# Row gathers by indirect DMA in the gated experts of a three-layer model, conditioning in blocks of 1024 columns, and the overflow loop at the head of its stage

## The chip, the cores and the metric

One core of a Trainium2 chip runs the whole program. The metric is the device time of one execution in microseconds, lower is better. The kernel before takes 2925.19 us (median of 3 runs, 2920.35 to 2933.56).

## What is computed

512 tokens of width 1024 go through three layers. Each has a mixer over the sequence (RWKV-7 with gated linear attention, then RG-LRU with Hyena, then a conformer convolution) and, after it, a mixture of experts (MoE). The first MoE has 32 experts of width 512; each token takes two of them. The later two have 16 experts of width 1024, and there each expert chooses its 64 tokens:

```python
def _ec_moe(h, router, w1, w3, w2):
    probs = jax.nn.softmax(jnp.einsum('bnd,de->ben', h, router), axis=1)
    gates, idx = lax.top_k(probs, cap)           
    xs = h[bidx, idx]
    a = jnp.einsum('becd,edf->becf', xs, w1)
    g = jnp.einsum('becd,edf->becf', xs, w3)
    y = jnp.einsum('becf,efd->becd', jax.nn.silu(a) * g, w2) * gates[..., None]
    return jnp.zeros_like(h).at[bidx, idx].add(y)
```

The input `h` of these two is a normalised row times `1 + scale` plus `shift`. Scale, shift and an output gate come from the conditioning vector: `silu(c) @ w_mod + b_mod`, a 1024 by 6144 matrix for each of the two later layers. All arithmetic is float32.

## The kernel before

The program is written against a tile framework. It emits operations in program order, and a scheduler puts them into one fixed list per engine; an engine runs its own list strictly in order and waits on semaphores. Emission order is the priority, so that an operation emitted late fills places where earlier ones would wait by the scheduler's reckoning. Below, SP is the engine whose queue issues the weight loads, and POOL (GpSimd) issues the software DMAs and the gathers.

The stages in the profiled run: the first mixer until about 640 us (`phase1`; it also has the conditioning, as filler work), the first MoE until about 1335 (`moe1`; it also has the Hyena `filters` and the context recurrence, `context`, as filler), the second mixer until about 1640, the MoE of the first later layer until 2168.5 (`moe2`), the third mixer until 2380, and the MoE of the second later layer until about 2908.

**Conditioning** (`adaln_block`, L909 to L945). 48 blocks of 256 columns; each is two loads of 512 KB into `wm` (2 buffers), eight matmuls at L921 into four column groups of the array, a copy at L923, and one more matmul step with `sel` that adds up the four groups (L931 for gate rows, L937 for scale and shift). Among the blocks, `zeros` clears a `wm` tile and writes it nine times into the region of `yslot` (a DRAM table of expert outputs) that belongs to slots which nobody fills: one DMA of 4.6 MB on POOL's queue, L348.

**The first MoE** works in 16 pairs of experts. `tokens` (L1636) computes for two pairs at a time which token sits in which slot: one-hot (`oh`), eight small matmuls (`tr`, L1743), a reduction and a cast on VectorE (L1745, L1746). `rows_load` (L1748) then gathers 128 rows of `xrow` (normalised rows in DRAM) by one indirect DMA on POOL (`xg`, 512 KB, L1752) and transposes them on TensorE (`gat` and `cb`, L1757). `ffn` runs the gate and up products `G` (L1519), the transposes `tr` (L1529) and the down product `Y` (L1539). An expert with more than 64 tokens is finished in `overflow` (L1931), a hardware loop whose count is read at run time; in the profiled run the count is zero. It stands before pair 4, with nine weight tiles loaded ahead (`self.ahead(9)`), and the filters just before it. A hardware loop is entered by all engines together, once all DMAs in flight have landed.

**The later MoEs** work in four quads, each of two pairs of experts. `experts` (L1811) builds the one-hot `oh` of a quad. `gather` (L1488) multiplies all 512 normalised rows by it, 64 matmuls of 256 columns at L1496; the rows are held in SBUF as two parts, `xhi` and `xlo`, 16 KB each per partition, so that their sum is exact, and the result is already transposed; an activation (L956) applies scale and shift. Per pair follow the slots' gates (`slot_gates`, L1731), the transposed one-hot `ohT` (L1828), `ffn`, and `outputs` (L1773), which multiplies by the gate and spreads the result back to the tokens by `cb` matmuls (L1796) with `yhi` and `ylo`, and adds them to `xres`.

**Weights** come in tiles of 1 MiB through a ring of buffers; a load (`ring`, L1449) is issued from SP's queue when a buffer is free. A pair of the later MoEs takes 24 loads: 16 for `G`, 8 for `Y`; a layer takes 192. Ring of the later MoEs: 6 tiles that are there before the mixer's memory is free and 9 behind (5 and 10 in the last layer), 15 in all. `moe_open` and `ring_open` lay it out. Two names of the list below: an fp32 matmul with 512 columns in an engine's list (`G`, `Y`) is two instructions in the trace; `gat`, `cb` and the transposes are one.

Of the kernel before, what the change touches and what calls it, by code (L numbers as in the profile page):

```python
# [10 lines left out]
F32 = mybir.dt.float32  # L11
# [9 lines left out]
T, D = 512, 1024  # L21
# [158 lines left out]
class Kern:  # L180
# [57 lines left out]
    def phase1(self, _):  # L238
# [4 lines left out]
        with ExitStack() as es:  # L243
# [82 lines left out]
            def shifted(ft, out):  # L326
# [14 lines left out]
            self.adaln_setup(P, "glo")  # L341
            fills = (self.adaln_block(l, cb, lambda: P([128, 1024], "wm", bufs=2), lambda: bank("ad"), lambda: P([128, 256], "rows", bufs=2))
                     for l in range(2) for cb in range(24))
            def zeros():

                z = P([128, 1024], "wm", bufs=2)
                nc.gpsimd.memset(z, 0.0)
# [8 lines left out]
            fill(24)  # L356
            self.rwkv_pair(1, **X)
            gl(6)
            fill(10)
            self.rwkv_pair(2, **X)  # L360
            self.rwkv_pair(3, **X)
            fill(12)
# [501 lines left out]
    def norm_tile(self, M, W, bank, t, wr, ps_):  # L864
        nc, V = self.nc, self.nc.vector
        x = self.xres[:, t]
        hi, lo = (M.xn[t],) * 2 if M.rows else (M.hi[:, t], M.lo[:, t])
# [9 lines left out]
        nc.scalar.activation(lo, x, AF.Square, accum_out=rs)  # L877
        nc.scalar.activation(rs, rs, AF.Sqrt, scale=1.0 / D, bias=self.eps)
        V.reciprocal(rs, rs)
        if M.rows:  # L880
            V.scalar_tensor_tensor(hi, x, rs, M.lnrow, op0=OP.mult, op1=OP.mult)
            nc.gpsimd.dma_start(self.xrow[128 * t:128 * t + 128], hi)
            return
        nc.scalar.activation(hi, x, AF.Copy, scale=rs)
        V.scalar_tensor_tensor(lo, x, rs, hi.bitcast(F32), op0=OP.mult, op1=OP.subtract)
# [9 lines left out]
    def adaln_setup(self, p, tag="sel4"):  # L895
# [6 lines left out]
        sel4 = p([128, 128, 4], tag)[:, 0:32]  # L902
        nc.gpsimd.memset(sel4, 1.0)
        nc.gpsimd.affine_select(out=sel4, in_=sel4, pattern=[[-1, 32], [-32, 4]], compare_op=OP.is_equal, fill=0.0,
                                base=0, channel_multiplier=1)
        self.sel = p([128, 32], "sel")
        nc.vector.tensor_reduce(self.sel, sel4, axis=AX.X, op=OP.add)

    def adaln_block(self, l, cb, w4, bank, row):  # L909

        nc, c = self.nc, self.col
        ws = []
        for g in range(2):
            w = w4().rearrange("p (k n) -> p k n", k=4)
            nc.sync.dma_start(w, self.A["w_mod"][l, 512 * g:512 * g + 512, 256 * cb:256 * cb + 256]
                              .rearrange("(k p) n -> p k n", p=128))
            ws.append(w)
        ps = bank()
        for g in range(2):
# [3 lines left out]
        nc.scalar.copy(rows, ps[:, 0:256])  # L923
        j, part = divmod(cb, 4)
        ps = bank()
        if j in (2, 5):
            q = 2 * l + (j == 5)
            g = row()[0:1]
            z = self.gates[q:q + 1, 256 * part:256 * part + 256]
            nc.gpsimd.dma_start(g, self.A["b_gate"][q:q + 1, 256 * part:256 * part + 256])  # L930
            nc.tensor.matmul(ps[0:32, 0:256], self.sel, rows, start=True, stop=True)  # L931
            nc.vector.tensor_add(g, g, ps[0:1, 0:256])
            nc.gpsimd.dma_start(z, g)
            return
        p2 = ps[:, 0:4].rearrange("p (a b) -> p a b", b=2)
        for a in range(2):
            nc.tensor.matmul(p2[:, a], rows[:, 128 * a:128 * a + 128], self.sel[:, 0:2], start=True, stop=True)  # L937

        where = {0: 1, 1: 0, 3: 3, 4: 2}[j] + 6 * l
        todo = [(where, 0, j)]  # L940
        if l == 0 and j < 2:
            todo.append((4 + (j == 0), 1, j))
        for slot, m, j in todo:
            o = self.mods[:, slot, 2 * part:2 * part + 2]
            nc.vector.tensor_add(o, p2[:, :, m], c(f"b_mod{l}{j}", 2 * part, 2))  # L945
            if j in (1, 4):
                n = c(f"norm{1 if j == 1 else 2}_g_2{l}", 2 * part, 2)
# [540 lines left out]
    def gather(self, P, bank, hi, lo, oh, n, affine):  # L1488

        nc = self.nc  # L1490
        xT = P([128, KT, 256], "xT")[:, :, 0:n]
        for k in range(KT):
            ps = bank("gat", 1)[:, 0:n]
            for t in range(NT):
                for m, part in enumerate((hi, lo)):
                    nc.tensor.matmul(ps, part[:, t, 128 * k:128 * k + 128], oh[:, t], start=t == 0 and m == 0,  # L1496
                                     stop=t == NT - 1 and m == 1)
            affine(xT[:, k], ps, k)
        return xT

# [43 lines left out]
    def moe1(self, yT):  # L1544
        nc, tc, A = self.nc, self.tc, self.A
        with ExitStack() as es:
            c = self.col
            M, bank = self.moe_open(es, "m1", "right", True)
            self.ring_open(es, 9, "right")
            ring = self.rings[0][0]  # L1550
            M.xn = [z for i in range(2) for z in tiles(ring([128, 2, D], "w", bufs=9))]
            self.rings = [(ring, "w", 7, 9)]
# [14 lines left out]

            self.rings = self.rings + [(P, "w", 2, 2), (ring, "w", 2, 9)]
# [74 lines left out]

            tokens(0)

# [36 lines left out]
            def over():  # L1682
                self.ahead(9)
                self.overflow(P, B, bank, s1, s12, pend)

            bk = lambda: bank("bg", 1)
            for pair in range(15):
                if pair % 2 == 0 and pair < 14:
                    tokens(pair // 2 + 1)
                if pair == 4:  # L1690
                    self.filters(B, bk)
                    over()
                z = slice(128 * pair, 128 * pair + 128)
                self.rows_ffn(P, bank, self.rows_load(P, bank, tok[:, pair:pair + 1], 128), self.yslot[z], self.take, 2)
# [21 lines left out]
            for t in range(NT):  # L1716
                for n in range(2):
# [3 lines left out]
                    V.tensor_add(self.xres[:, t, z], self.xres[:, t, z], ps)  # L1721
            self.context(B, bk)

    def slot_gates(self, P, bank, oh, m, cols):

        nc = self.nc
        g = P([128, 1], "gate", bufs=2)
        ps = bank("tr", 1)
        for e in range(m // 64):
            for t in range(NT):  # L1730
                nc.tensor.matmul(ps[64 * e:64 * e + 64, 0:1], oh[:, t, 64 * e:64 * e + 64].bitcast(F32), cols(t, e),  # L1731
                                 start=t == 0, stop=t == NT - 1)
        nc.scalar.copy(g[:m], ps[:m, 0:1])
        return g
# [13 lines left out]
    def rows_load(self, P, bank, tok, m):  # L1748

        nc, V = self.nc, self.nc.vector  # L1750
        xg = P([128, D], "xg", bufs=3)[:m]
        nc.gpsimd.indirect_dma_start(xg, None, self.xrow[:], bass.IndirectOffsetOnAxis(ap=tok, axis=0))  # L1752
        xT = P([128, KT, 128], "xT", bufs=2)[:, :, 0:m]
        for b in range(2):
# [3 lines left out]
            (V.tensor_copy if b else nc.scalar.copy)(xT[:, 4 * b:4 * b + 4], ps)  # L1758
# [52 lines left out]
    def experts(self, P, bank, hi, lo, R, cm, affine, ne, ff, g2, at={}):  # L1811

        nc, V = self.nc, self.nc.vector
        for quad in range(ne // 4):
            if quad in at:
                at[quad]()
# [232 lines left out]
```

## Time and profile before

| | |
|---|---|
| median of 3 runs | 2925.19 us |
| the profiled execution | 2929.81 us, span 2928.2 us |
| TensorE busy | 2551.1 us (87%), mean granted clock 0.934 |
| VectorE, ScalarE, GpSimd busy | 38%, 23%, 3% of the span |
| DMA | 765.9 MB, mean 262 GB/s |
| bytes on the software queue (POOL's) | 28.92 MB |

Read it by stage: a mean over the span mixes stages in which the DMA engines stand half idle (the mixers) with stages in which they move about 400 GB/s without a pause (the MoEs). "Idle before, releaser" tells how long an engine stood idle before an instruction and what ended it. The granted clock is given as a share of full speed: 1.00 is 2.4 GHz, 0.50 is 1.2 GHz.

### The profile page before, as it was taken

How to read it: one execution, taken by the hardware profiler on the slowest of the kernel's cores; microseconds unless marked ns; L12 is line 12 of the kernel's file. 1: busy time of each engine (PE TensorE's matmuls, PEld its weight loads, DVE VectorE, ACT ScalarE, POOL GpSimd, SP SyncE). 2: the span in 40 equal slices, each digit the busy share in tenths (PEclk: the TensorE clock that was granted, in tenths of full speed). 3: DMA queues.
4: the chain of work that ended last, by engine and by line, in shares of the span. 5: the costliest groups of instructions: out<-in, count | busy, mean ns of one | idle time of the engine just before them, and what ended most of it. 6: DMA issues, size and time to landing. Idle time of an engine off the chain costs nothing.

```text
span 2928.2 us, 37470 instructions
## 1 busy us (share of the span) xinstructions
PE 2551.1 (87%) x15670; PEld 1395.8 (48%) x15670; DVE 1109.9 (38%) x2099; ACT 672.9 (23%) x1092; POOL 87.2 (3%) x169
## 2 busy tenths in 40 slices
PE   7989999867996988868889699999989669999997
PEld 3565756655433444435566533333347553333333
DVE  3857576734211230014776411111138651111113
ACT  3233323322101350004631211011024321101101
POOL 1000000000110000010000000000000000000000
PEclk9988999878998999988999799999999779999999
DMA  4345343137989999993133399999953238999987
GB/s 148 110 165 191 100 143 125 59 110 269 351 325 345 397 349 394 397 398 127 58 121 118 138 397 400 409 382 409 379 206 128 90 151 350 401 409 382 409 330 295
DMA packets 277963, 765.90 MB, mean 262 GB/s; under 512 B 15579, under 2 KB 66011, under 8 KB 276896
## 3 DMA queue, kind: packets, MB, share of 16 engines
q1 hardware_dynamic: 260480, 711.77, 64.4%
q0 software_dynamic: 8992, 28.92, 2.5%
q10 hardware_dynamic: 8320, 22.80, 2.2%
q8 instruction: 124, 2.03, 0.3%
q14 instruction: 47, 0.39, 0.0%
HBM read 740.34 MB, written 23.09 MB: 261 GB/s over the span
## 4 chain that ended last, share of the span: by engine, by line
PE 48%; DVE 8%; issue 5%; DMA 4%; ACT 3%; POOL 0%; DVEq 0%; POOLq 0%; ACTq 0%; SPq 0%
PE G L1519 19%; PE Y L1539 12%; PE b L1222 4%; PE gat L1496 3%; PE cb L1796 3%; PE G L809 2%; PE Y L809 2%; DMA xg<-xrow,tok 1%; DVE cy L1391 1%; PE tr L1529 1%; DMA w<-in_moe_w_up_dram 1%; DVE h L1524 1%; DMA yo<-yslot,slot 1%; PE tr L876 1%; PE b L1341 0%
## 5 line engine op out<-in xcount | busy, mean ns | idle before, releaser
L1519 PE MATMUL G<-w,xT 128*64 128x256 f32 (+1 forms) x4096 | 745.0, 496 | 17.9 <-DMA w<-in_moe_w_up_dram 11.8
L1519 PEld LDWEIGHTS G<-w,xT 128*64 128x64 f32 x4096 | 291.1, 138 | 375.1 <-issue 289.4
L1539 PE MATMUL Y<-w,hT 128*64 128x512 f32 x1536 | 452.1, 603 | 2.4 <-DMA w<-in_moe_w_down_dram 1.3
L1539 PEld LDWEIGHTS Y<-w,hT 128*64 128x64 f32 x1536 | 148.1, 137 | 227.3 <-issue 210.7
L1524 DVE TENSOR_TENSOR h<-h,G 128x256 f32<-128x256 f32 (+1 forms) x64 | 35.3, 552 | 530.1 <-PE G L1519 394.7
L1787 DVE SCALAR_TENSOR_TENSOR y<-Y,gate,g 128x512 f32<-128x512 f32 x32 | 24.0, 751 | 331.7 <-PE Y L1539 330.1
L1798 DVE TENSOR_TENSOR xres<-xres,cb 128x512 f32<-128x512 f32 x116 | 79.6, 686 | 101.0 <-PE cb L1796 101.0
L321 PE MATMUL mm<-hT,w 128*128 128x512 f32 x240 | 113.7, 609 | 0.0
L1523 ACT ACTIVATE h<-G 128x256 f32<-128x256 f32 (+1 forms) x64 | 31.4, 490 | 301.0 <-PE G L1519 288.9
L956 ACT ACTIVATE xT<-gat,mods 128x256 f32<-128x256 f32 x64 | 36.1, 563 | 247.4 <-PE gat L1496 207.2
L1222 PE MATMUL b<-big,wh 128*128 128x512 f32 x320 | 83.9, 414 | 5.6 <-ACT wh L861 3.0
L1530 ACT COPY hT<-tr 128x256 f32<-128x256 f32 (+1 forms) x64 | 30.6, 478 | 243.8 <-PE tr L1529 243.8
L921 PE MATMUL ad<-wm,sc 128*32 128x256 f32 x768 | 68.0, 416 | 18.7 <-DMA wm<-in_w_mod_dram 15.9
L1496 PE MATMUL gat<-oh,xhi 128*128 128x256 f32 x256 | 75.1, 321 | 7.7 <-ACT xT L956 4.0
L1788 ACT CAST yhi<-y 128x512 fp32r<-128x512 f32 x30 | 18.5, 618 | 265.6 <-DVE y L1787 164.0
L1496 PEld LDWEIGHTS gat<-oh,xhi 128*128 128x128 f32 x256 | 50.9, 199 | 51.0 <-issue 29.2
L1222 PEld LDWEIGHTS b<-big,wh 128*128 128x128 f32 x320 | 62.7, 198 | 23.5 <-ACT big L1203 6.4
L1796 PEld LDWEIGHTS cb<-yhi,ohT 128*128 128x128 f32 x114 | 21.2, 186 | 103.0 <-DVE xres L1798 56.8
L1496 PE MATMUL gat<-oh,xlo 128*128 128x256 f32 x256 | 67.9, 295 | 0.0
L643 PE MATMUL g<-wb,hT 128*64 128x128 f32 x1024 | 64.5, 275 | 3.5 <-DVE ga L718 2.1
L321 PEld LDWEIGHTS mm<-hT,w 128*128 128x128 f32 x240 | 42.3, 190 | 48.3 <-issue 47.4
L1796 PE MATMUL cb<-yhi,ohT 128*128 128x512 f32 x114 | 56.9, 499 | 9.7 <-ACT yhi L1788 9.7
(684 smaller groups left out, 3700.4 us busy)
## 6 DMA issues: line engine op xcount, KB each, us to landing
w<-in_exp_w_dram SPq DMA_DIRECT2D x384, 1024.0 KB, 12.7
w<-in_moe_w_gate_dram SPq DMA_DIRECT2D x64, 1024.0 KB, 15.4
w<-in_moe_w_up_dram SPq DMA_DIRECT2D x64, 1024.0 KB, 15.3
w<-in_moe_w_down_dram SPq DMA_DIRECT2D x64, 1024.0 KB, 13.9
wm<-in_w_mod_dram SPq DMA_DIRECT2D x96, 512.0 KB, 4.3
ws<-in_w_in_dram SPq DMA_DIRECT2D x20, 512.0 KB, 3.5
ws<-in_cf_w_dram SPq DMA_DIRECT2D x20, 512.0 KB, 3.5
st<-in_w_out_dram SPq DMA_DIRECT2D x16, 512.0 KB, 4.6
```

The lines of the kernel that those rows point to most:

```text
L321: nc.tensor.matmul(ps[:m], w[:, k, col0:col0 + m], hT[:, k], start=k == 0, stop=k == KT - 1)
L643: nc.tensor.matmul(ps[half[h], b], hT[:, k, 64 * j:64 * j + 64], w[h][:, k], start=k == 0, stop=k == KT - 1)
L809: nc.tensor.matmul(ps, a[:, k, z], b[:, k % 2], start=k == 0 and m == 0, stop=k == KT - 1 and m == 2)
L921: nc.tensor.matmul(ps[32 * k:32 * k + 32, 0:256], self.sc[:, 4 * g + k], ws[g][:, k], start=g == 0, stop=g == 1)
L956: self.nc.scalar.activation(out, ps, AF.Identity, scale=a, bias=b)
L1222: nc.tensor.matmul(ps, a[:, k], b[:, k], start=m == 0 and k == 0, stop=m == 2 and k == KT - 1)
L1496: nc.tensor.matmul(ps, part[:, t, 128 * k:128 * k + 128], oh[:, t], start=t == 0 and m == 0, stop=t == NT - 1 and m == 1)
L1519: nc.tensor.matmul(parts[m][64 * c:64 * c + 64], xT[:, k, 64 * e:64 * e + 64], w[:, kk, H * c:H * c + H], start=k == 0, stop=k == KT - 1)
L1524: nc.vector.tensor_mul(h, h, parts[1])
L1539: nc.tensor.matmul(ys[n][64 * e:64 * e + 64], hTs[e][:, f], ws[e][:, ff_, 512 * n:512 * n + 512], start=f == 0, stop=f == nf - 1)
L1796: nc.tensor.matmul(ps, ohT[:m, 128 * t:128 * t + 128], p[k][:m], start=k == 0, stop=k == 1)
L1798: V.tensor_add(xr, xr, ps)
```

## The change

There are three parts.

**The later experts gather rows by DMA.** `norm_tile` writes the normalised rows to `xrow` in DRAM (four POOL DMAs of 512 KB per layer) as the first MoE's already did, and `xhi` and `xlo` are gone. A new `prepare(pair)` computes the slots' token numbers and gates together (eight matmuls of three columns, a reduction, a cast), gathers 128 rows by indirect DMA, transposes them (8 transposes), applies scale and shift in 8 small operations (4 on ScalarE, 4 on VectorE), and builds `ohT`. It is called for the next pair ahead of `ffn`. The ring has 10 early tiles in place of 6 (9 for 5), of which two hold the rows until they are written, and 7 behind (8): 17 tiles in all.

**Conditioning in 12 blocks of 1024 columns**: eight loads of 512 KB each, each with four matmuls into the four column groups, which now hold four ranges of columns rather than four parts of a sum. So L931's step is gone, and L937's is 8 blocks of two matmuls.

**The first MoE**: the zeros are written just before `tokens(0)`, pair 0's rows are loaded before the loop, the loop stands before pair 0 with eleven tiles loaded ahead, and `filters` is emitted behind the pairs, just before `context`.

```diff
-            fills = (self.adaln_block(l, cb, lambda: P([128, 1024], "wm", bufs=2), lambda: bank("ad"), lambda: P([128, 256], "rows", bufs=2))
-                     for l in range(2) for cb in range(24))
-            def zeros():
...
-                nc.gpsimd.dma_start(self.yslot[1920:].rearrange("(a p) d -> p a d", p=128), z[:, None].to_broadcast([128, 9, 1024]))
-
-            fills = itertools.chain(itertools.islice(fills, 8), (zeros() for _ in range(1)), fills)
+            fills = (self.adaln_block(l, j, lambda: P([128, 1024], "wm", bufs=2), lambda: bank("ad"), lambda: P([128, 256], "rows", bufs=2))
+                     for l in range(2) for j in range(6))
...
-        for g in range(2):
-            for k in range(4):
-                nc.tensor.matmul(ps[32 * k:32 * k + 32, 0:256], self.sc[:, 4 * g + k], ws[g][:, k], start=g == 0, stop=g == 1)
+        for k in range(KT):
+            w = w4()
+            nc.sync.dma_start(w, self.A["w_mod"][l, 128 * k:128 * k + 128, D * j:D * j + D])
+            for g in range(4):
+                nc.tensor.matmul(ps[32 * g:32 * g + 32, 0:256], self.sc[:, k], w[:, 256 * g:256 * g + 256], start=k == 0,
+                                 stop=k == KT - 1, tile_position=(0, 32 * g))
...
+            z = P([128, D], "xg", bufs=3)
+            nc.gpsimd.memset(z, 0.0)
+            nc.gpsimd.dma_start(self.yslot[1920:].rearrange("(a p) d -> p a d", p=128), z[:, None].to_broadcast([128, 9, 1024]))
             tokens(0)
+            xT0 = self.rows_load(P, bank, tok[:, 0:1], 128)
...
-            def over():
-                self.ahead(9)
-                self.overflow(P, B, bank, s1, s12, pend)
-
+            self.ahead(11)
+            self.overflow(P, B, bank, s1, s12, pend)
...
-                if pair == 4:
-                    self.filters(B, bk)
-                    over()
...
+            self.filters(B, bk)
             self.context(B, bk)
...
+            ps = bank("bg", 1)
+            for e in range(2):
                 for t in range(NT):
...
+                    nc.tensor.matmul(ps[64 * e:64 * e + 64, 0:3], oh[:, t, e].bitcast(F32), gt[:, t, 2 * pair + e],
+                                     start=t == 0, stop=t == NT - 1)
+            g, tok = P([128, 2], "gate", bufs=3), P([128, 1], "tok", I32, bufs=2)
+            V.tensor_reduce(g[:, 1:2], ps[:, 1:3], axis=AX.X, op=OP.add)
+            V.tensor_copy(tok, g[:, 1:2])
+            nc.scalar.copy(g[:, 0:1], ps[:, 0:1])
+            xT = self.rows_load(P, bank, tok, 128, affine)
+            ps = bank("bg", 1)
...
+        nxt = prepare(0)
+        for pair in range(ne // 2):
+            xT, g, ohT = nxt
+            if 2 * pair + 2 < ne:
+                nxt = prepare(pair + 1)
+            ys = self.ffn(P, bank, xT, self.take, 2, ff)
+            self.outputs(P, bank, ys, g, 128, g2, ohT, 2 * pair + 2 == ne)
```

**Where instructions stand now.** TensorE's list of the kernel before, in the `Y` product of a pair whose next quad is gathered beside it (`Y` uses the weights `w` and the transposed hidden rows `hT`; `gat` gathers by `oh`):

```order
L1496 MATMUL gat_11572<-oh_11549,xlo_10550 128x256
L1828 MATMUL tr_11643<-identr_78,oh_11549 128x128 x3
L1539 MATMUL Y_11455<-w_11469,hT_11389 64x512
L1539 MATMUL Y_11456<-w_11469,hT_11389 64x512
L1496 MATMUL gat_11582<-oh_11549,xhi_10549 128x256
L1496 MATMUL gat_11582<-oh_11549,xlo_10550 128x256
L1496 MATMUL gat_11582<-oh_11549,xhi_10549 128x256
L1496 MATMUL gat_11582<-oh_11549,xlo_10550 128x256
L1496 MATMUL gat_11582<-oh_11549,xhi_10549 128x256
L1496 MATMUL gat_11582<-oh_11549,xlo_10550 128x256
L1496 MATMUL gat_11582<-oh_11549,xhi_10549 128x256
L1496 MATMUL gat_11582<-oh_11549,xlo_10550 128x256
```

The gather's matmuls stand in eights between the steps of `Y`. TensorE's list of the changed kernel, in the `G` product of the third pair: the slots' numbers (`bg<-gt,oh`), `ohT` (`bg<-identr,oh`), and the first half of the transposes of the gathered rows (`gat<-ident,xg`); the rows `xg_11558` are those whose numbers the third row here computes.

```order
L1716 MATMUL cb_11312<-ident_72,xg_11300 128x128 x4
L1493 MATMUL G_11329<-w_11354,xT_11046 64x512 x3
L1789 MATMUL bg_11544<-gt_10725,oh_11542 64x3 x8
L1493 MATMUL G_11329<-w_11360,xT_11046 64x512 x4
L1798 MATMUL bg_11579<-identr_78,oh_11542 128x128 x4
L1493 MATMUL G_11329<-w_11366,xT_11046 64x512 x4
L1716 MATMUL gat_11561<-ident_72,xg_11558 128x128 x4
L1493 MATMUL G_11329<-w_11372,xT_11046 64x512 x4
L1503 MATMUL tr_11381<-ident_72,h_11378 128x128 x4
```

So between the numbers of a pair's tokens and the first instruction that reads the gathered rows stand eight matmuls of `G` and the four of `ohT`; the second half of the transposes (`cb<-ident,xg`) stands one pair later, and `Y` is 32 matmuls with nothing between. Each of the six gathers behind the first two has such a place; the first of them has six `cb` matmuls there as well.

POOL's list of the kernel before at the head of the first MoE (`xrow` are the normalised rows being written, `cpad` belongs to the context recurrence, `xg` are pair gathers):

```order
L882 DMA xrow<-w_5416 128x1024 x2
L882 DMA xrow<-w_5417 128x1024
L994 MEMSET cpad_8842 128x1
L995 MEMSET cpad_8842 128x2
L994 MEMSET cpad_8861 128x1
L995 MEMSET cpad_8861 128x2
L882 DMA xrow<-w_5417 128x1024
L1752 DMA xg_5979<-xrow,tok_5914 128x1024
L1752 DMA xg_6122<-xrow,tok_5914 128x1024
```

The same place in the changed kernel; `ovi` is the loop's count.

```order
L877 DMA xrow<-w_5138 128x1024 x2
L877 DMA xrow<-w_5139 128x1024
L1615 MEMSET xg_5637 128x1024
L981 MEMSET cpad_8567 128x1
L982 MEMSET cpad_8567 128x2
L981 MEMSET cpad_8586 128x1
L982 MEMSET cpad_8586 128x2
L1616 DMA yslot<-xg_5637 128x9x1024
L877 DMA xrow<-w_5139 128x1024
L1711 DMA xg_5654<-xrow,tok_5636 128x1024
L1929 TENSOR_LOAD ovi_5731
L1930 COMPARE_AND_BRANCH
```

The clearing of a tile and the write of zeros now stand ahead of the last write of `xrow` and of pair 0's gather, and the loop follows that gather; in SP's list it follows the eleventh weight load.

## Rows read from the trace of the kernel before

**Rows 1.** Windows: us, PE, PEld, DVE, ACT, POOL busy (x), PEclk, DMA share, GB/s

```profile
0.00:640.00 640.00, 556.81 (x6160) 365.52 (x6160) 394.47 (x890) 196.64 (x340) 27.65 (x65) 0.91 0.38 122
...
640.00:1335.00 695.00, 582.92 (x3341) 309.66 (x3342) 160.63 (x338) 138.58 (x235) 56.14 (x72) 0.93 0.94 351
...
1640.00:2168.50 528.50, 484.44 (x2146) 191.47 (x2146) 94.59 (x151) 55.89 (x99) 0.00 (x0) 0.97 0.94 370
...
2380.00:2908.00 528.00, 483.84 (x2150) 191.84 (x2150) 93.94 (x150) 55.89 (x99) 0.00 (x0) 0.97 0.94 373
```

**Rows 2.** Windows: two pairs of the first later layer, and all eight

```profile
1733.10:1802.45 69.35, 66.83 (x295) 26.73 (x296) 8.75 (x14) 8.85 (x16) 0.00 (x0) 1.00 1.03 409
1802.45:1860.60 58.15, 55.26 (x246) 20.09 (x248) 10.82 (x16) 4.34 (x8) 0.00 (x0) 1.00 1.01 398
...
1684.30:2168.50 484.20, 464.77 (x2045) 176.97 (x2044) 72.77 (x104) 48.61 (x87) 0.00 (x0) 1.00 0.97 383
```

**Rows 3.** Groups by line in 1684.3 to 2168.5: busy us, mean ns | idle before

```profile
L1496 PE MATMUL gat<-oh,xhi 128*128 128x256 f32 x103 | 28.7, 308 | 2.0 <-ACT xT L956 2.0
...
L1496 PE MATMUL gat<-oh,xlo 128*128 128x256 f32 x104 | 26.3, 286 | 0.0
```

**Rows 4.** Timeline of TensorE: start us, us, instruction [idle before <-releaser]

```profile
1733.05 1.94 PE L1519 MATMUL G<-w,xT 128*64 128x512 f32 x8
...
1752.31 0.63 PE L1529 MATMUL tr<-ident,h 128*128 128x128 f32 x4 [0.94 <-DVE h L1524]
...
1778.03 0.45 PE L1828 MATMUL tr<-identr,oh 128*128 128x128 f32 x3
```

**Rows 5.** Windows: end of that layer's experts, a stretch of the first MoE

```profile
2123.00:2150.00 27.00, 26.15 (x114) 8.69 (x114) 3.96 (x6) 2.36 (x4) 0.00 (x0) 1.00 1.03 410
2150.00:2168.50 18.50, 17.64 (x80) 8.88 (x76) 1.44 (x2) 0.58 (x1) 0.00 (x0) 1.00 0.11 44
...
1100.00:1320.00 220.00, 172.31 (x1091) 90.28 (x1088) 25.79 (x39) 15.93 (x37) 14.93 (x18) 0.92 1.04 397
```

**Rows 6.** The row gather of the first MoE (L1752), 16 of them

```profile
DMA to landing us min/median/max: 7.0/7.9/12.6
```

**Rows 7.** Timeline of the first MoE, all engines, columns as above

```profile
1113.66 0.16 DVE L1746 CAST tok<-toks 128x2 int32<-128x2 f32 x1
...
1114.57 0.99 POOL L1752 DMA_INDIRECT xg<-xrow,tok  x1 [18.48 <-issue]
...
1121.71 1.11 PE L1757 MATMUL gat<-ident,xg 128*128 128x128 f32 x4 [5.67 <-DMA xg<-xrow,tok]
```

**Rows 8.** Windows around that wait, granted clock in the column PEclk

```profile
1118.00:1120.00 2.00, 0.00 (x0) 0.00 (x0) 0.00 (x0) 0.00 (x0) 0.00 (x0) 0.90 1.05 396
...
1124.00:1126.00 2.00, 2.00 (x6) 0.52 (x4) 0.00 (x0) 0.00 (x0) 0.00 (x0) 0.50 1.06 389
1126.00:1128.00 2.00, 2.00 (x11) 0.76 (x8) 0.00 (x0) 0.19 (x1) 0.00 (x0) 0.90 1.03 384
```

**Rows 9.** Groups by line in 0 to 640 (conditioning)

```profile
L937 PE MATMUL ad<-sel,rows 128*128 128x2 f32 x128 | 18.4, 248 | 0.5 <-ACT rows L923 0.5
...
L931 PE MATMUL ad<-rows,sel 128*32 128x256 f32 x32 | 12.1, 467 | 1.1 <-ACT rows L923 1.0
```

**Rows 10.** Waits of TensorE in 0 to 640: us in total, times, longest

```profile
PE ad L921 <- DMA wm<-in_w_mod_dram: 15.9, 9, 7.6
```

**Rows 11.** DMA issues: line engine op xcount, KB each, median us to landing

```profile
yslot<-wm POOLq DMA_DIRECT2D x1, 4608.0 KB, 18.6
```

**Rows 12.** Window at the first MoE's loop

```profile
870.00:915.00 45.00, 20.69 (x51) 8.00 (x49) 7.83 (x11) 4.89 (x8) 4.93 (x5) 0.77 0.77 279
```

**Rows 13.** A shorter window at its head

```profile
700.00:705.00 5.00, 2.29 (x20) 2.09 (x18) 3.37 (x11) 1.95 (x5) 0.73 (x5) 0.82 0.07 20
```

**Rows 14.** Timeline of GpSimd at the first MoE's head

```profile
704.07 0.53 POOL L882 DMA_DIRECT2D xrow<-w  x1 [1.47 <-DVE w L881]
714.95 1.05 POOL L1752 DMA_INDIRECT xg<-xrow,tok  x1 [10.35 <-DMA w<-in_moe_w_up_dram]
```

More of the change, by code (lines that the diff above doesn't have):

```diff
@@ L866, in norm_tile @@
         x = self.xres[:, t]
-        hi, lo = (M.xn[t],) * 2 if M.rows else (M.hi[:, t], M.lo[:, t])
+        xn = M.xn[t]
         rs = M.rs[:, t:t + 1]
@@ L876, in norm_tile @@
             nc.tensor.matmul(ps_[:, t], xT[:, k], wr[:, k], start=k == 0, stop=k == KT - 1)
-        nc.scalar.activation(lo, x, AF.Square, accum_out=rs)
+        nc.scalar.activation(xn, x, AF.Square, accum_out=rs)
         nc.scalar.activation(rs, rs, AF.Sqrt, scale=1.0 / D, bias=self.eps)
         V.reciprocal(rs, rs)
[L880 to L885, printed above, removed]
+        if M.lnrow is None:
+            nc.scalar.activation(xn, x, AF.Copy, scale=rs)
+        else:
+            V.scalar_tensor_tensor(xn, x, rs, M.lnrow, op0=OP.mult, op1=OP.mult)
+        nc.gpsimd.dma_start(self.xrow[128 * t:128 * t + 128], xn)
     def router(self, M, ps, c, n):
@@ L922, in adaln_block @@
         rows = row()
-        nc.scalar.copy(rows, ps[:, 0:256])
-        j, part = divmod(cb, 4)
-        ps = bank()
         if j in (2, 5):
             q = 2 * l + (j == 5)
[L928 to L933, printed above, removed]
+            b = row()
@@ L934, in adaln_block @@
+            for g in range(4):
+                nc.gpsimd.dma_start(b[32 * g:32 * g + 1], self.A["b_gate"][q:q + 1, 256 * g:256 * g + 256])
+            for g in range(4):
+                z = slice(32 * g, 32 * g + 1)
+                nc.vector.tensor_add(rows[z], b[z], ps[z, 0:256])
+                nc.gpsimd.dma_start(self.gates[q:q + 1, 256 * g:256 * g + 256], rows[z])
             return
-        p2 = ps[:, 0:4].rearrange("p (a b) -> p a b", b=2)
+        nc.scalar.copy(rows, ps[:, 0:256])
@@ L1486, in weights @@
                     yield rows(w2, e, 2, i)
[L1488 to L1499, printed above, removed]
     def ffn(self, P, bank, xT, take, ne, ff):
@@ L1547, in moe1 @@
             c = self.col
[L1548 to L1552, printed above, removed]
+            M, bank = self.moe_open(es, "m1", "right", 9, A["ln2_row"])
             self.nbuf = 2
@@ L1834, in moe_open, with prepare @@
-    def moe_open(self, es, name, side, rows=False):
+        def prepare(pair):
+            if pair % 2 == 0:
+                oh = self.oh = P([128, NT, 4, 64], "oh", F32R)
+                V.tensor_tensor(oh, R[:, :, 2 * pair:2 * pair + 4, None].to_broadcast([128, NT, 4, 64]),
+                                self.iota[:, None, None, 0:64].to_broadcast([128, NT, 4, 64]), op=OP.is_equal)
+            oh = self.oh[:, :, 2 * (pair % 2):2 * (pair % 2) + 2]
+            ps = bank("bg", 1)
+            for e in range(2):
+                for t in range(NT):
+                    nc.tensor.matmul(ps[64 * e:64 * e + 64, 0:3], oh[:, t, e].bitcast(F32), gt[:, t, 2 * pair + e],
[6 more added lines that the diff above has]
+            ps = bank("bg", 1)
+            for t in range(NT):
+                nc.tensor.matmul(ps[:, 128 * t:128 * t + 128], oh[:, t].rearrange("p e s -> p (e s)"), self.identr, start=True,
+                                 stop=True)
+            ohT = P([128, T], "ohT", F32R, bufs=2)
+            nc.scalar.copy(ohT, ps)
+            return xT, g[:, 0:1], ohT
@@ L1884, in moe2 @@
             self.close_y()
[L1885 removed]
             P = Pool(es.enter_context(tc.tile_pool(name=f"m2b{l}", bufs=1, side="right")))
[L1887 removed]
+            ring = Pool(es.enter_context(tc.tile_pool(name=f"ring{Pool.count}", bufs=1, side="right")))
+            self.ring_more(M, (ring, "w", 7 + l, 7 + l))
             g2 = P([128, D], "g2")
```

124 lines of the change are left out of this document (46 added, 78 removed).

## The prediction

> **What bounds the kernel now.** I read the windows by stage first [rows 1]. The two later MoEs take 528 us each and are alike: TensorE is busy for 484 us of both, and the DMA engines stand at a share of 0.94. So both are near their limit there, and what the change takes from TensorE can be earned only as far as the weights follow. In the first MoE the DMA share is 0.94 as well, with TensorE busy for 583 of 695 us: there the bytes count. In the first 640 us DMA has a share of 0.38 and TensorE is busy for 557 us: there TensorE counts, with VectorE's 394 us beside it.
>
> Inside the first later MoE the windows of single pairs [rows 2] show what the one-hot gather costs: a pair beside which the next quad is gathered takes 69.35 us, one without 58.15. All eight take 484.2 us, 464.8 of them busy. The end of the stage [rows 5] tells which engine is late: DMA runs at 410 GB/s up to 2150 and then has nothing left, while TensorE needs 18.5 us more to use up what the ring holds. TensorE sets the end, by less than 20 us.
>
> **The later MoEs, term by term.** Removed: in these 484.2 us, 103 and 104 gather matmuls, 28.7 + 26.3 = 55.0 us busy [rows 3]. Added: six of the eight gathers fall into this stretch, each with eight transposes; four transposes take 0.63 us [rows 4], so 48 take 7.6 us. The slots' matmuls and `ohT` are as many as before. Busy time becomes 464.8 - 55.0 + 7.6 = 417.4 us. Of the idle 19.4 us, 2.0 belonged to the gather [rows 3]; 17.4 stay. Sum without new waits: 434.8 us.
>
> The change also adds a wait, and the lists show where: the transposes `gat<-ident,xg` stand in TensorE's list close behind the matmuls that compute the token numbers, and all of `G` behind them is held up when the rows aren't there. TensorE's work in between is two steps of eight `G` instructions at 1.94 us and four of `ohT` (three take 0.45) [rows 4]: 4.5 us. The chain beside it can be read in the first MoE, which has the same one [rows 7]: a cast of 0.16 us, a reduction that I take for as long, 0.75 us from the cast's end (1113.82) to the gather's issue at 1114.57, and 7.14 us from there to the transposes at 1121.71. That is 8.2 us, so TensorE stands for 3.7 us. (There it stood 5.67.) The sixteen gathers of the first MoE landed after 7.0 to 12.6 us, median 7.9 [rows 6]; I take 7.14, as the ring is nearer to full here than there. The pause also costs clock: in the case read, the granted clock fell from 1.00 to 0.50 just before 1120 and came back after 1126 [rows 8], some 4.5 us of work at half rate behind the return at 1121.71, or 2.2 us lost. [...] So 6.0 us each for five gathers, and 3 us for the one with six more `cb` matmuls in between: 33 us. The second half of the transposes stands a pair later and waits for nothing.
>
> The sum is 434.8 + 33 = 468 us against 484.2: 16 us less. The bounds of a gather's wait are 0 us (rows land in time) and 12.6 + 1.1 - 4.5 + 2.2 = 11.4 us.
>
> What would be late next is DMA. 17 tiles stand ready at the first `G` in place of 15, so 175 loads of 1 MiB follow, 2.56 us each at 410 GB/s [rows 5]: 448 us. Six gathers of 512 KB take 1.28 us each of the same engines, 8 us, then 2 us until the first buffer is free and 4 us for the last product: 462 us, or 22 us less than now. At 397 GB/s, the rate of the stretch of the first MoE that also has gathers and stores [rows 5], it is 476 us, 8 us less. So TensorE with its pauses (468) lies between the two; I keep 16 us.
>
> Ahead of the first `G` 64 gather matmuls go, 17 us by the 55.0 us for 207 [rows 3]; 8.2 us of chain, the slots' matmuls and the transposes take their place, some 11 us, at a clock that the pause has lowered. I take 0; bounds -6 and +3. The writes of `xrow` lie in the router's time, where DMA waits for buffers. For two layers: 33 us less, bounds 44 less and 38 more (68 us of waits in 434.8 + 68 = 503).
>
> The Trainium skill, "DMA: Bandwidth & Descriptors", section "Anatomy of one DMA — SWDGE (gpsimd) path", fits a software DMA by 2.0 us plus its bytes at 436 GB/s, an estimate of 3.2 us for 512 KB; the gathers here took 7.0 us at least [rows 6], so the trace disagrees, and with 3.2 us there would be no pause at all. The same page's "Rules for kernel authors" advises to issue a DMA early and to wait late, which this list does only for half of the transposes.
>
> **Conditioning.** L931 goes, 12.1 us in 32 instructions; L937 falls from 128 instructions to 32, 18.4 us to 4.6 [rows 9]. The matmuls with `w_mod` and their loads stay as they are. 26 us of TensorE work go, but much of it is filler: TensorE is idle for 83 of the 640 us [rows 1]. I take half, 13 us. The waits for `wm`, 15.9 us, the longest of 7.6 [rows 10], stood beside the write of zeros that held a `wm` buffer for 18.6 us [rows 11]; without it that one goes, but a block now draws eight loads through two buffers one behind the other, so I book nothing. Bounds: 27 us less, 8 more.
>
> **The first MoE.** The loop no longer cuts the stream. In 870 to 915 TensorE is busy for 20.7 of 45 us and DMA has a share of 0.77 against 1.04 [rows 12, 5]: 45 x 0.27 / 1.04 = 12 us of transfer, and transfer is what counts afterwards. At the head the price stands. The zeros are issued behind the `cpad` clears, just ahead of the fourth write of `xrow` at 704 [rows 14], while DMA is idle (0.07 [rows 13]); 4.6 MB take 11.5 us at 410 GB/s, 18.6 beside other loads [rows 11]. Pair 0's gather, issued at 715 [rows 14], lands behind them at about 730 instead of 724, and the loop's entry waits for it and for eleven loads and then drains the engines: some 9 us later to the first `G`. The filters move from full TensorE time before the loop to places among pairs 3 to 6; I book nothing. Net 3 us less; bounds 12 less (the head is covered) and 12 more (18.6 us of zeros in full, and half the loop's gain lost).
>
> **How the sum stands.** 33 + 13 + 3 = 49 us off the profiled execution's 2929.8: 2881. It was 4.6 us above the median, so the median becomes 2876.
>
> **Rivals.**
> - *The rows land before TensorE asks.* They must land within 4.5 - 1.1 = 3.4 us of issue. For it: TensorE now lags, so buffers may stay full and DMA stand idle. Against it: 7.0 us is the least in [rows 6]. DMA then sets the end: 2 x 22 + 16 = 60 off, 2865. This is where the skill's fit of 3.2 us would lead.
> - *DMA at 397 GB/s sets the end.* For it: gathers and writes now run in these stages, as in the first MoE. Against it: 409 GB/s in a pair here [rows 2]. 2 x 8 + 16 = 32 off: 2893.
> - *The first two parts give nothing*, the head of the first MoE costing 12 us and conditioning staying filler: 33 - 12 = 21 off, 2904.
> - *Slower: the gather's wait outgrows what the one-hot products cost.* The gathers go into a full stream, land after 12.6 us, TensorE drops to half clock each time: 11.4 us for each of six, 19 us more per layer, 38 - 16 = 22 us more, 2947. It decides from 2 x (434.8 + 6 w - 484.2) = 16, a wait of w = 9.6 us per gather, that is a landing of 10.8 us.
>
> **How the numbers follow.** Forecast 0.40; rows in time 0.14; DMA at 397 GB/s 0.20; first parts nothing 0.14; slower 0.12. The low end takes the second case with the full bounds of the first two parts, 44 + 27 + 12 = 83 off: 2842. The high end, 2920, leaves out the slower rival's upper part. 0.5% is 14.6 us, about what a measurement of this kernel can tell from no change. Faster by more: 0.38 + 0.14 + 0.18 + 0.07 = 0.77; within: 0.02 + 0.02 + 0.07 + 0.03 = 0.14; slower: 0.09.
>
> **What would show it.** In the later MoEs: `Y` without interruption; about six waits per layer of TensorE for `xg`, of 3 to 4 us, with windows at half clock behind them; eight pairs in some 468 us. In the first MoE: no gap near 900, one of some 30 us before the first `G` near 737. Until 640: 10 to 15 us less. It is wrong if the waits for `xg` are over 9 us, or if the DMA share in the experts falls well under 0.97 without them.

## The result

The changed kernel takes 2885.43 us (median of 4 runs, 2873.63 to 2891.01) against 2922.80 us for the kernel before on the same chip: a ratio of 0.9862, 95% interval 0.9834 to 0.9889. That is 37 us less, 2876 was forecast, 2842 to 2920 given as the range. The profiled execution takes 2891.0 us, 39 us less than that of before.

The stages of both profiles, by the first write of `xrow` (the first MoE begins), the end of its last `Y`, the router's result (`R`) and the last `Y` of both later MoEs. Times in us from the span's start:

| | first `xrow` | end of first MoE | `R` | end | `R` | end | span |
|---|---|---|---|---|---|---|---|
| before | 678.4 | 1332.1 | 1666.9 | 2168.5 | 2407.5 | 2909.1 | 2928.2 |
| after | 649.9 | 1303.3 | 1637.8 | 2135.5 | 2375.1 | 2869.5 | 2889.4 |
| earlier by | 28.5 | 28.8 | 29.1 | 33.0 | 32.4 | 39.6 | 38.8 |

So in these two executions 28.5 us come from the first stage, nothing from the first MoE, 4 and 7 us from the later MoEs. The total is near the forecast; its parts are not: 13, 3 and 33 were forecast.

**The later MoEs.** The waits stand where the lists had them. The changed kernel's timeline of TensorE, the first half of two pairs' transposes (start us, us, instruction [idle before <-releaser]):

```profile
1707.46 1.11 PE L1716 MATMUL gat<-ident,xg 128*128 128x128 f32 x4 [4.24 <-DMA xg<-xrow,tok]
...
1798.60 1.11 PE L1716 MATMUL gat<-ident,xg 128*128 128x128 f32 x4 [4.38 <-DMA xg<-xrow,tok]
```

All of them from the first `G` to the last `Y` (us in total, times, longest):

```profile
PE gat L1716 <- DMA xg<-xrow,tok: 27.8, 6, 5.7
```

Six waits of 4.2 to 5.7 us, 4.6 on average, where 3.7 was forecast ([rows 7] show 5.67 in the first MoE of the kernel before). One of these gathers in POOL's timeline:

```profile
1791.11 0.95 POOL L1711 DMA_INDIRECT xg<-xrow,tok  x1 [64.50 <-DVE tok L1793]
```

From the issue to the transposes at 1798.60 it is 7.49 us, against the 7.14 taken [rows 7]; the wait of 4.38 us began at 1794.22, 3.1 us after the issue. And the clock fell. Windows around that wait (us, TensorE, weight loads, VectorE, ScalarE, GpSimd busy, granted clock, DMA share, GB/s):

```profile
1794.00:1796.00 2.00, 0.22 (x2) 0.00 (x0) 0.00 (x0) 0.00 (x0) 0.00 (x0) 1.00 1.04 416
...
1798.00:1800.00 2.00, 1.40 (x6) 1.01 (x8) 0.00 (x0) 0.00 (x0) 0.00 (x0) 0.50 1.03 412
...
1804.00:1806.00 2.00, 1.81 (x6) 1.01 (x8) 0.14 (x1) 0.59 (x1) 0.00 (x0) 0.50 0.99 371
1806.00:1808.00 2.00, 2.00 (x8) 0.62 (x6) 0.00 (x0) 0.00 (x0) 0.00 (x0) 0.56 0.95 379
```

TensorE stops at 1794.2; the clock goes from 1.00 to 0.50 just before 1798 and is back only near 1808, some 9 us after the work began again, not 4.5 [rows 8]. `Y` is free of interruptions, as forecast. From the first `G` to the last `Y` of the layer:

```profile
1649.30:2135.50 486.20, 438.70 (x1884) 173.00 (x1883) 83.87 (x146) 44.03 (x88) 5.68 (x6) 0.95 0.97 385
```

and in the kernel before:

```profile
1676.50:2168.50 492.00, 472.57 (x2085) 181.13 (x2084) 72.77 (x104) 51.34 (x92) 0.00 (x0) 1.00 0.96 378
```

34 us of busy time are gone and 28 us of idle time have come. In addition busy time now holds work at half rate: added up over windows of 2 us, busy time times one minus granted clock gives 17.2 us here (13.4 in the second layer), and nothing before. At full rate the work would be 421 us; the forecast's 417.4 is for a stretch that begins 7.8 us later.

**The first stage.** L931 is gone; of L937's step this is left, and the waits for `wm` are 3 us longer than before in total, though none is as long as the longest there [rows 9, 10]:

```profile
L923 PE MATMUL ad<-sel,rows 128*128 128x8 f32 x32 | 5.0, 259 | 0.0
```

```profile
PE ad L907 <- DMA wm<-in_w_mod_dram: 19.1, 19, 3.8
```

TensorE's work until the first `xrow`, clock taken out in the same way, fell from 544.9 to 525.2 us. Its idle time stayed (86.5 and 89.5 us), and the time lost to half clock fell from 47.1 to 35.1 us.

**The first MoE.** At its head the write of zeros costs more than forecast. The changed kernel's timeline, all engines:

```profile
675.11 1.02 POOL L1616 DMA_DIRECT2D yslot<-xg  x1 [0.16 <-POOL cpad L982]
...
676.12 0.58 POOL L877 DMA_DIRECT2D xrow<-w  x1
...
703.41 1.05 POOL L1711 DMA_INDIRECT xg<-xrow,tok  x1 [26.70 <-issue]
709.46 1.09 PE L1716 MATMUL gat<-ident,xg 128*128 128x128 f32 x4 [19.39 <-DMA xg<-xrow,tok]
...
715.18 2.82 PE L1493 MATMUL G<-w,xT 128*64 128x256 f32 x10 [2.07 <-issue]
```

```profile
yslot<-xg POOLq DMA_DIRECT2D x1, 4608.0 KB, 26.2
```

The zeros are issued at 675.11 and the last `xrow` write behind them; the zeros land 26.2 us after their issue, where the forecast took 11.5 to 18.6. The gather of pair 0 needs that last `xrow` write and is issued only at 703.41, though its token numbers were ready by 686 (it could be issued 11 us after the last write before [rows 14], 27 us here). From the first `xrow` to the first `G` it is now 65.3 us, 48.2 before; behind the first `G` the stage takes 588 us instead of 605. The place where the loop had cut the stream still loses transfer:

```profile
870.00:915.00 45.00, 45.00 (x223) 19.51 (x224) 7.97 (x13) 7.53 (x15) 3.09 (x3) 1.00 0.80 281
```

DMA has a share of 0.80 there, 0.77 before [rows 12]. But TensorE, busy for 20.7 us then, is now busy for all 45: the filters stand here, and the buffers stay full. So the transfer that the loop cost at this place was not won back here.

### The profile page after: what moved, and what is told of

The parts are those of the page before. It is cut to its first block, busy times and chain, and to the rows that moved or that the text cites. A ratio compares the mean times of both kernels' runs of the same rounds, so it can differ in the third digit from the quotient of the medians.

```text
span 2889.4 us, 36529 instructions
## 1 busy us (share of the span) xinstructions
PE 2454.6 (85%) x15158; PEld 1352.8 (47%) x15158; DVE 1124.1 (39%) x2143; ACT 643.5 (22%) x1049; POOL 107.0 (4%) x193
## 5 line engine op out<-in xcount | busy, mean ns | idle before, releaser
L1493 PE MATMUL G<-w,xT 128*64 128x256 f32 (+1 forms) x4096 | 772.4, 507 | 22.5 <-DMA w<-in_moe_w_up_dram 18.1
L1513 PE MATMUL Y<-w,hT 128*64 128x512 f32 x1536 | 402.7, 602 | 2.6 <-DMA w<-in_moe_w_down_dram 1.3
L1513 PEld LDWEIGHTS Y<-w,hT 128*64 128x64 f32 x1536 | 172.2, 137 | 195.3 <-issue 182.6
L1498 DVE TENSOR_TENSOR h<-h,G 128x256 f32<-128x256 f32 (+1 forms) x64 | 35.4, 553 | 516.8 <-PE G L1493 406.8
L1716 PE MATMUL gat<-ident,xg 128*128 128x128 f32 x128 | 30.4, 371 | 95.4 <-DMA xg<-xrow,tok 95.3
L1751 ACT CAST yhi<-y 128x512 fp32r<-128x512 f32 x30 | 18.6, 619 | 310.5 <-DVE y L1750 224.2
L1716 PEld LDWEIGHTS gat<-ident,xg 128*128 128x128 f32 x128 | 19.1, 183 | 117.9 <-DMA xg<-xrow,tok 88.2
L1503 PE MATMUL tr<-ident,h 128*128 128x128 f32 x192 | 35.8, 297 | 39.1 <-DVE h L1498 39.0
L1711 POOL DMA_INDIRECT xg<-xrow,tok x32 | 31.1, 972 | 887.6 <-DVE tok L1793 435.7
```

The costliest lines, as they stand in the source:

```text
L1493: nc.tensor.matmul(parts[m][64 * c:64 * c + 64], xT[:, k, 64 * e:64 * e + 64], w[:, kk, H * c:H * c + H], start=k == 0, stop=k == KT - 1)
L1498: nc.vector.tensor_mul(h, h, parts[1])
L1503: nc.tensor.transpose(ps[:, j].rearrange("p c s -> p (c s)"), h[:, 128 * j:128 * j + 128], self.ident)
L1513: nc.tensor.matmul(ys[n][64 * e:64 * e + 64], hTs[e][:, f], ws[e][:, ff_, 512 * n:512 * n + 512], start=f == 0, stop=f == nf - 1)
L1716: nc.tensor.transpose(ps[:, k], xg[:, 512 * b + 128 * k:512 * b + 128 * k + 128], self.ident[:m, :m])
```

## The experiments

Each ratio is against the kernel before on the same chip. One program can differ between chips and sessions: the kernel of the fourth experiment, run twice, gave 0.9774 and 0.9806. The times of single stages are those of one profiled execution each.

**The three parts, one at a time.** First the conditioning alone, with the zeros in a `wm` buffer as before:

```diff
...
-                     for l in range(2) for cb in range(24))
+                     for l in range(2) for j in range(6))
...
-            fills = itertools.chain(itertools.islice(fills, 8), (zeros() for _ in range(1)), fills)
+            fills = itertools.chain(itertools.islice(fills, 2), (zeros() for _ in range(1)), fills)
...
-            fill(24)
+            fill(7)
...
```

> The kernel before with the conditioning in blocks of 1024 columns alone; the zeros stay in the first stage, in a wm buffer. The profile of the changed kernel reached the first write of xrow 28.5 us earlier than that of the kernel before. Theory: the blocks did most of it (19 us of TensorE work are gone, and with them some half-clock time): about 20 us less than before, the first write of xrow near 658. Rival: it was the removal of the zeros, which held a wm buffer and made TensorE wait 7.6 us: then at most 10 us less here.

0.9920 (0.9903 to 0.9937), 23 us less; the first `xrow` at 647.3. TensorE's work until then is 524.6 us, idle 88.6, lost to half clock 34.1. The theory holds: the blocks do it, and the rival falls, since the zeros are still there. The profile shows 31 us, more than the whole time: 20 of them are work, and most of the rest is half clock, which differs between executions.

Then the first MoE's changes alone:

```diff
...
-            fills = itertools.chain(itertools.islice(fills, 8), (zeros() for _ in range(1)), fills)
...
+            nc.gpsimd.dma_start(self.yslot[1920:].rearrange("(a p) d -> p a d", p=128), z[:, None].to_broadcast([128, 9, 1024]))
             tokens(0)
+            xT0 = self.rows_load(P, bank, tok[:, 0:1], 128)
...
+            self.ahead(11)
+            self.overflow(P, B, bank, s1, s12, pend)
...
+            self.filters(B, bk)
             self.context(B, bk)
```

> The kernel before with the changes to the first MoE alone (zeros written at its head, pair 0's rows before the loop, the loop ahead of pair 0, filters emitted last). Theory: the first MoE itself gains nothing (17 us more before its first G, as much less at the old place of the loop), and the first stage, without the zeros, some 8 us: about 8 us less. Rival of e1: the zeros were what cost in the first stage: about 20 us less or more.

0.9951 (0.9934 to 0.9967), 14 us less, between both. The first `xrow` stands at 662.6, 16 us earlier than in the kernel before and 9 earlier than in the next experiment, whose first stage is that of the kernel before (671.8). Only 6 us of this are idle time (80.2 against 86.5 and 86.0); the rest is time at half clock (36.4 against 47.1 and 41.4), so what the zeros cost there beside the small blocks is shown for 6 us and not for the rest. From there to the end of the first MoE it takes 660.2 us, 6.5 more than before.

Then the gathers alone (`experts`, `norm_tile`, the rings; first stage and first MoE's order as before):

```diff
...
-            xT = self.gather(P, bank, hi, lo, oh, 256, affine)
...
+            xT = self.rows_load(P, bank, tok, 128, affine)
...
```

> The kernel before with the row gathers of the later MoEs alone. Theory, by the two traces: 4 us less in the first later layer, 7 in the second, so about 11 us less. Rival: the gain as predicted, 33 us less, part of which the other two changes gave back.

0.9955 (0.9941 to 0.9969), 13 us less. From `R` to the end both layers take 495 us against 501.6: 6.5 us less each. TensorE waits 27.8 us for `xg` in the first of them. So the theory holds, and the gathers alone have the waits too. The three ratios multiply to 0.983, the whole has 0.986; the intervals are too wide to tell the two apart. That the gain of the zeros' place can't be had twice would fit, and is not shown.

**The wait taken away.** In the changed kernel the scheduler can't put the token matmuls earlier: they share a PSUM bank (`bg`) with those of `ohT`, whose result waits there until one of two `ohT` buffers is free. One more buffer:

```diff
-            ohT = P([128, T], "ohT", F32R, bufs=2)
+            ohT = P([128, T], "ohT", F32R, bufs=3)
```

> The changed kernel with a third buffer for ohT and nothing else. The scheduler then puts the matmuls for the token numbers far ahead of the transposes of the gathered rows, with dozens of G and Y steps between. Theory: the waits for xg (28 us a layer) and the half clock behind them (13 to 17 us) go, until DMA sets the pace: 15 to 20 us less per layer, 30 to 40 in all against the changed kernel, 2845 to 2855. Rival: DMA sets the pace already and the waits turn into waits for weights: 0 to 8 us less.

0.9774 (0.9758 to 0.9791); the median is 2857.4 us, 28 us below the changed kernel's (26 us by the ratios). `R` to end: 483.4 and 483.0 us, 14 and 11 us less than in the changed kernel. The longest of TensorE's waits in the first layer, from `R` on (no load of weights is among them), and the layer's windows:

```profile
PE gat L1716 <- DMA xg<-xrow,tok: 14.5, 7, 5.0
PE tr L1503 <- DVE h L1498: 13.7, 16, 0.9
```

```profile
1638.60:2110.50 471.90, 438.31 (x1884) 175.58 (x1883) 83.41 (x146) 44.03 (x88) 5.68 (x6) 0.98 1.00 396
1800.00:1900.00 100.00, 92.13 (x372) 38.15 (x370) 20.42 (x35) 9.34 (x20) 1.89 (x2) 0.98 1.03 409
...
2095.00:2110.50 15.50, 15.28 (x68) 8.31 (x68) 0.92 (x2) 0.59 (x1) 0.00 (x0) 1.00 0.60 240
```

28.5 us of waits became 14.5, of which 9 stand in the second pair; the time lost to half clock fell from 17 to 6 us. That is 25 us, but from the first `G` to the last `Y` the layer is only 14 us shorter: TensorE's busy time stayed at 438 us. The difference is `G`. Its group in the changed kernel, and here:

```profile
L1493 PE MATMUL G<-w,xT 128*64 128x512 f32 x1024 | 259.5, 627 | 0.0
L1493 PE MATMUL G<-w,xT 128*64 128x512 f32 x1024 | 261.1, 608 | 0.0
```

Some 13 us of the first figure and 4 of the second are half clock, so that at full clock `G` takes 11 us longer here. In the new list the steps of `cb`, `gat` and `bg` stand between `G`'s instructions in more places. These start in twos, within 0.01 us of each other, and such a pair takes 0.43 us; one without a partner takes as long, and there are 82 of those here, 34 in the changed kernel.

DMA runs at 409 GB/s over long stretches, but TensorE doesn't wait for it: all of the last `Y` runs without a pause, while DMA has little left to do.

```profile
2095.81 14.69 PE L1513 MATMUL Y<-w,hT 128*64 128x512 f32 x64
```

In the second layer TensorE waits once for a load, 0.6 us. So neither the theory's limit nor the rival's is what was met: DMA stands close behind, and TensorE still sets the pace. 14 and 11 us a layer lie below the 15 to 20 of the theory (its 2845 to 2855 is just missed) and above the 0 to 8 of the rival; what is missing are the waits that are left and the 11 us of `G`. The same kernel once more:

> The changed kernel with the third ohT buffer once more, as the neighbour of the kernel with two writes of zeros. Theory and rival: 2857 within 5 us; its first stage shows how far executions of one program differ there (the profiles so far ended it between 639 and 650 us).

0.9806 (0.9790 to 0.9822), 2866.1 us: 9 us above the 2857 expected, outside the 5 us given. `R` to end: 490.3 and 483.1 us; in the first layer 12 us were lost to half clock instead of 6. Against the changed kernel's ratio of 0.9862 the third buffer is worth 16 us by this run and 26 by the first. This kernel and the one with the early zeros (below, 2857.2 us) are the fastest of all, below both that of before and the changed one.

**The ring.** The same kernel with 15 tiles:

```diff
-            self.ring_more(M, (ring, "w", 7 + l, 7 + l))
+            self.ring_more(M, (ring, "w", 5 + l, 5 + l))
```

> The changed kernel with the third ohT buffer and two weight tiles fewer in the later MoEs, 15 as in the kernel before. With the third buffer DMA runs at 409 GB/s nearly to the end of the layer. Theory: DMA sets the pace there, so two loads that are not done ahead cost 2.56 us each: 5 us per layer, 10 in all, 2867. Rival: TensorE sets the pace: no change, 2857.

0.9830 (0.9805 to 0.9856). `R` to end: 487.7 and 488.9 us, 4.3 and 5.9 more than in the fourth experiment's first profile (two loads of 2.56 us each are 5.1), but 2.6 less and 5.8 more than in its second. The whole is above both of them by ratio, 0.9774 and 0.9806; from the second alone the difference would not be told. At the first layer's end, the window and a piece of the last `Y`:

```profile
2095.00:2120.70 25.70, 23.61 (x92) 8.20 (x88) 1.49 (x3) 1.63 (x2) 0.00 (x0) 1.00 0.89 358
```

```profile
2111.98 4.49 PE L1513 MATMUL Y<-w,hT 128*64 128x512 f32 x16 [0.63 <-DMA w<-in_exp_w_dram]
```

From 2095 to the layer's end DMA works at 358 GB/s, above at 240. And now the last `Y` waits for loads: twice, 1.2 us in all, and `Y`'s instructions take 121 us of the layer instead of 118. Together that is about the 4.3 us. So with 15 tiles DMA does set the layer's end, and with 17 not yet; that two loads cost just their transfer time fits, and is not shown to a microsecond.

**The first MoE's three moves**, all on the kernel with the third buffer. The zeros in the first stage again:

```diff
...
+            fills = itertools.chain(itertools.islice(fills, 2), (zeros() for _ in range(1)), fills)
...
-            nc.gpsimd.dma_start(self.yslot[1920:].rearrange("(a p) d -> p a d", p=128), z[:, None].to_broadcast([128, 9, 1024]))
             tokens(0)
```

> The changed kernel with the third ohT buffer, and the zeros written in the first stage again (a wm buffer, after two of the twelve conditioning blocks). In the changed kernel the first write of xrow and the first G of the first MoE lie 65 us apart, 48 in the kernel before: the write of 4.6 MB stands ahead of the last write of xrow and of pair 0's gather. Theory: that is the price of the zeros at the head; here the distance falls to some 53 us, the first stage gets no longer (it did not in the run with the conditioning alone), and since bytes set the pace of the first MoE, about 10 us less than with the third buffer alone, 2847. Rival: the head's price is the loop's entry (it waits for eleven loads): no change, 2857.

0.9777 (0.9753 to 0.9801), 2857.2 us: the whole is the same, not 10 us less. From the first `xrow` to the first `G` it is 57.6 us instead of 65.6, to the end of the first MoE 645.3 instead of 653.2. So the zeros at the head cost 8 us, not all 17; the rest goes with the loop's entry, as the loop's move below shows. Whether the early write costs the first stage as much as it saves is told by writing them at both places:

```diff
...
+            fills = itertools.chain(itertools.islice(fills, 2), (zeros() for _ in range(1)), fills)
...
```

> The changed kernel with the third ohT buffer, and the zeros written twice: in the first stage (through a wm buffer, as with early zeros) and at the head of the first MoE. The early zeros took 8 us from the first MoE, and the whole time stayed as it was. Theory: their write costs about 8 us in the first stage as well: 8 us more than the same kernel with the third buffer alone, run beside it. Rival: it is free there, and the 8 us were a difference between executions: within 3 us.

0.9796 (0.9777 to 0.9815), 2866.3 us, with 2866.1 us for its neighbour without the early zeros (0.9806). The rival holds by the whole time: in the first stage the write is free within what these runs can tell, though the two profiles' first stages differ by 6 us (650.9 against 644.8). In the profiled execution without the late zeros the 8 us were hidden by a longer first stage (647.5 against 639.4 us). How much the early zeros gain in the whole time is not settled by these runs: nothing to 8 us.

The loop before pair 4 again, on top of the early zeros:

```diff
-            self.ahead(11)
-            self.overflow(P, B, bank, s1, s12, pend)
...
+                if pair == 4:
+                    self.ahead(9)
+                    self.overflow(P, B, bank, s1, s12, pend)
```

> As the kernel with early zeros, but the overflow loop stands before pair 4 again, with nine tiles loaded ahead. Theory: the loop in the middle of the stream costs the 12 us of transfer that I read in the kernel before, while the head without it is some 6 us shorter: 6 us more than with early zeros alone. Rival: the loop's place doesn't matter, within 3 us.

0.9788 (0.9766 to 0.9811), 2864.0 us: 7 us above the kernel with early zeros by the medians, 3 by the ratios, too little to tell theory from rival. The head is 46.8 us instead of 57.6, the first MoE 647.4 instead of 645.3: 2 us more, as the rival has it. So the loop costs 11 us at the head; in the stream the part behind the first `G` is 13 us longer. Not all of these need be the loop's: most of the filters' matmuls now run from 900 to 1046 us instead of 740 to 899. At the loop:

```profile
820.00:850.00 30.00, 1.88 (x8) 1.57 (x8) 1.22 (x1) 0.59 (x1) 3.37 (x3) 0.50 0.89 335
```

Here TensorE stands for 28 of 30 us, and DMA has 0.89 where a share of 1.04 is full: some 4 us of transfer. Where the other 9 go was not found.

The filters ahead of pair 4, on top of the early zeros:

```diff
+                if pair == 4:
+                    self.filters(B, bk)
...
-            self.filters(B, bk)
             self.context(B, bk)
```

> As the kernel with early zeros, but the filters are emitted ahead of pair 4 instead of behind the pairs. Theory: I booked nothing for their place: within 4 us of the kernel with early zeros. Rival: emitted earlier, they crowd TensorE in the first pairs and buffers stay full: 8 us more or above.

0.9814 (0.9792 to 0.9835); 12 us more in the medians, and the first MoE takes 653.3 us instead of 645.3. The rival's figure came, and I had booked nothing. Its mechanism is not shown: most of the filters' matmuls run from 740 to 878 us here and from 740 to 899 with the early zeros alone, and DMA falls behind mainly after them (a share of 1.00 from 940 to 1000 and 0.98 from 1000 to 1100, where it is 1.04 in the other).

## Why the prediction came out, step by step

- **That TensorE stays the engine that sets the later MoEs, with a wait for `xg` in six places per layer: right.** It was read from the list (token matmuls eight `G` steps before the transposes) and from the same chain in the first MoE. The rival "rows land before TensorE asks" has fallen: 7.5 us from issue, not 3.4. So has, for these gathers, the Trainium skill's fit that led there, an estimate of 3.2 us for 512 KB (the Trainium skill, "DMA: Bandwidth & Descriptors", section "Anatomy of one DMA — SWDGE (gpsimd) path"). The gathers here ran beside loads that filled the engines (share 1.0).
- **The size of that term was wrong: 33 us forecast for both layers, 11 measured** (13 where it stood alone). The step that failed is the charge per wait, 6.0 us, and with it the 33 a layer. Measured were 27.8 us of waits and 17.2 lost to clock in the first layer, 45 together, and 28.8 and 13.4 in the second, 42. The pause was longer by 0.9 us on average. The wait with six `cb` in between was hardly shorter than the others (4.24 us), as its gather took 8.3 us from issue to the transposes. And the half rate lasted twice as long as in the single case that I took it from. In the first layer, 4 us less instead of 16, the shortfall of 12 adds up so: 12 us of waits and clock above the charge, 6 of idle time and work above the sum, 2 at the head (the first `G` stands 11.6 us behind `R` instead of 9.6), less 8, because my stretch of comparison began at 1684.3, when 8 us of `G` and gather had gone by. In the second layer the first of these is 9 us and the shortfall 9. Also wrong: of the 64 gather matmuls that I put ahead of the first `G`, 24 stand there.
- **Conditioning: 13 forecast, 28.5 measured here, 23 where it stood alone.** The step "much of it is filler, I take half" failed. 20 us of work went, not 26 (instructions' own times overlap); the idle 87 us did not change, so the length fell by all 20. The longest idle times that are not for `wm` are the same before and after (17.8 and 17.2 us, 10.1 and 10.0, 6.2 and 6.2): filler did not use them. The other 3 to 12 us are clock: less time at half rate, and in part chance, for two profiles of the first stage of the kernel before end at 678.4 and 671.8. The wait for `wm` of 7.6 us beside the zeros did vanish, others came, as the bounds had it.
- **The first MoE: 3 forecast, 0 measured; right in size, wrong in its parts.** The head cost 17 us, not 9, as the zeros took 26.2 us to land. Behind the first `G` 17 us came back, where 12 were forecast. The filters' place, on which nothing was booked, can decide 8.
- **The slower rival's condition, a wait of 9.6 us per gather with its clock, was met to three quarters:** 27.8 + 17.2 us over six gathers are 7.5 us in the first layer. With the first two parts giving the 16 us forecast, the gain would have been 27. The forecast's total owes its nearness to luck: the later MoEs gave 22 us less than forecast, the conditioning 15 more.
- **DMA as what comes next: near, and not reached by the third `ohT` buffer alone.** It took 472 us from first `G` to last `Y`, between the 462 at 410 GB/s and 476 at 397 of the prediction, but without a wait for weights in that layer. With two tiles fewer such waits appear.

## What to carry to other kernels

When an operation is replaced by a transfer, look in the engine's list for what stands between the instruction that starts the transfer's chain and the first that needs its data; if that is shorter than chain plus landing, the engine stops, and pays again in clock. Ask then which buffer keeps the scheduler from starting the chain earlier: here one more buffer of another tensor, 2 KB per partition, was worth 16 to 26 us. Look then at the whole list again: the same buffer moved other steps, and `G` became 11 us longer a layer. DMA at 409 GB/s did not yet set the pace here; a wait of TensorE for its data is what tells. And work taken from an engine that fills a stage counts in full, unless its idle time is shown to be time in which it could have run.

## What the runs showed of the hardware

The granted clock stayed at 0.50 for some 9 us after a wait of 4.4 us, while TensorE was busy for most of it, and for 4.5 us after one of 5.7 us in the kernel before [rows 8]. Executions of one program differ in this: four profiles of the kernels whose first stage is that of the changed kernel ended it at 639.4, 644.8, 647.2 and 649.9 us, with 26.9, 35.4, 38.5 and 35.1 us of busy time lost to half clock in the first 640 to 650 us. What decides where the clock falls within such a stage stays open.
